# Blocks of seven products: one sum of weight quadrants moved from VectorE to an accumulating transfer within SBUF

## The chip, the cores and the metric

The kernel runs on one core of a Trainium2 chip. The metric is device time in microseconds (us): the median of three runs. One execution was also taken by the hardware profiler. In it TensorE (PE) multiplies, VectorE (DVE) and ScalarE (ACT) do elementwise work, GpSimd (POOL) does a little of that and issues its own transfers, and SyncE (SP) issues the loads from HBM. Each engine runs its instructions in order and waits for the others by semaphores.

## The reference, cut to what matters

Two layers of a hybrid model on 512 tokens of width 1024, in float32. Each layer has a mixer (a gated one in the first layer, attention with forgetting in the second, each beside attention to a memory) and then a feed-forward part, which is where the change lies:

```
a = rmsnorm(h, ln_ffn_pre[layer])
f = silu(a @ w_ffn_gate[layer]) * (a @ w_ffn_up[layer])      # 1024 -> 2816
h = h + rmsnorm(f @ w_ffn_down[layer], ln_ffn_post[layer])   # 2816 -> 1024
```

## The kernel before

**Products in three parts.** A float32 operand is split in two parts, `hi` (a cast on ScalarE) and `lo` (what the cast left, a subtraction on VectorE); both come from `split`, and all splits have line L239. A product is three matmuls (`mm3`, L191 to L193): hi by hi, hi by lo and lo by hi in such an order that the third, L193, is the first to need the weights' `wlo`.

**Blocks of seven.** Most of the feed-forward products are done by a Strassen-like scheme: a 2x2 product of quadrants takes seven products in place of eight, and some additions of quadrants for it. `Seven` does it for a block of 256 columns of the gate or up weights. Its four weight quadrants a11, a12, a21, a22 are the halves of two loaded tiles `raw` (512 KB each, in a pool of four; each quadrant is 128x512 and 256 KB). `sums` makes s3 = a11 + a21 (L1041), then a21 + a22 (L1043), then from it a11 + a21 + a22 (L1045), then the last sum in a12 (L1046), each in place but for s3, and splits a11 and a12 in between, while they hold what was loaded. Products 1 to 7 are then run in the order 1, 7, 2, 6, 4, 3, 5, with the further splits in between (`run`). Product 7 uses s3 and is written to the PSUM tile `e`; products 1, 5 and 6 go to `a`, 2 and 3 to `x`, 4 to `e`. At the end (`end`) VectorE joins the results out of PSUM (L1079, L1080, L1082), which also frees those tiles.

`DownSeven` does the same for the down weights, whose sums are L1205 (s3), L1207 and L1208; half of these blocks have tiles `raw`, half four tiles `wd` of 256 KB.

**Groups.** A layer's 22 slices of 128 columns of gate and up are done as one plain pair and five groups. A group has two gate blocks and two up blocks in the order gate, up, gate, up. In the first group of a layer the first two are run with products 1, 2, 3 of the gate block, then of the up block, then the rest (`plain_first`), and the sums of all four blocks stand close together. After each of the first four groups come two `DownSeven` in `down_sevens`: eight transfers that accumulate onto the result tiles `y` in SBUF (`put`, L1234), and additions by VectorE (L1262, L1265, L1268). In layer 0 the inner groups open at about 262, 326, 390 and 450 us, in layer 1 at 844, 908, 970 and 1030. The first block of the next group is prepared while a group's down blocks run, so that the splits and sums of the one and the additions of the other stand mixed on VectorE.

**What sets the order.** A scheduler sets the order of instructions on each engine by priorities and modelled times; it keeps what depends on what. POOL's queue holds its transfers in order: the accumulates onto `y`, and those that finish the low part of `flo` (L1153), which are also accumulates of 256 KB within SBUF.

Of the kernel before, what the change touches and what calls it, by code (L numbers as in the profile page):

```python
# [11 lines left out]
ALU = mybir.AluOpType  # L12
# [28 lines left out]
def hybrid(ctx: ExitStack, tc: tile.TileContext, i: dict, out: bass.AP):  # L41
# [13 lines left out]
    def name(s):  # L55
        n_of[s] = n_of.get(s, 0) + 1
        return f"{s}_{n_of[s]}"
# [4 lines left out]
    def plain(s, shape=(P, T), dt=F32):  # L62
        return yp.tile(list(shape), dt, tag="y", name=name(s))

    def prob(s, shape=(P, T)):
        return tp.tile(list(shape), F32, tag="p", name=name(s), bufs=6)

    def temp(s, shape=(P, T), tag="t", bufs=4, dt=F32):
        return tp.tile(list(shape), dt, tag=tag, name=name(s), bufs=bufs)
# [4 lines left out]
    def ps(tag, shape=(P, T), s="ps"):  # L74
        return pp.tile(list(shape), F32, tag=tag, name=name(s), bufs=2 if tag == "tr" else 3)

    V, A, PE, G = nc.vector, nc.scalar, nc.tensor, nc.gpsimd
# [63 lines left out]
    def loaded(src):  # L141

        raw = wp.tile([P, 1024], F32, tag="raw", name=name("raw"), bufs=4)
        last_load[0] = nc.sync.dma_start(raw, src)
        return raw
# [116 lines left out]
    class Norm:  # L262


        def __init__(self, width=T):
            self.r4 = small("r4")
            self.acc, self.width = None, width
# [26 lines left out]
        def sums(self, tb, cols):  # L294
            return [self.acc[:, c + tb * P : c + (tb + 1) * P] for c in range(0, T, self.width)]
# [722 lines left out]
    class Seven:  # L1018
# [5 lines left out]
        def __init__(self, xs, src, tag, rows):  # L1024
            self.xs, self.rows = xs, rows
            w1, w2 = loaded(src(0)), loaded(src(1))
            self.a = [w[:, d : d + 512] for w in (w1, w2) for d in (0, 512)]
            self.x, self.p = ps(tag, s="x"), ps(tag, (P, 256), s="a")
            self.q = ps(tag, (P, 256), s="e")
            self.s1, self.s2 = prob("s1"), prob("s2")  # L1030
# [6 lines left out]
        def sums(self):  # L1037

            a11, a12, a21, a22 = self.a
            self.s3 = temp("s3")  # L1040
            V.tensor_add(self.s3, a11, a21)  # L1041
            self.w1 = self.parts(a11)
            V.tensor_add(a21, a21, a22)  # L1043
            self.w2 = self.parts(a12)
            V.tensor_add(a11, a21, a11)  # L1045
            V.tensor_add(a12, a11, a12)  # L1046

        def product(self, o, w, n, more=False):
# [64 lines left out]
    def feed_forward(layer, phase, xp, meanwhile=None):  # L1113
# [41 lines left out]
        class Inner:  # L1155

            def __init__(self, aside):
                self.aside, self.u = aside, {}
# [23 lines left out]
        class DownSeven:  # L1182

            def __init__(self, k, spare):
                if spare:
                    self.a = [plain("wd").rearrange("p (m c) -> p m c", m=4) for _ in range(4)]
                    for n, a in enumerate(self.a):
                        last_load[0] = nc.sync.dma_start(
                            a, i["w_down"][layer, 4 * (n // 2) : 4 * (n // 2) + 4, :, k + n % 2, :].rearrange("m p c -> p m c"))
                else:  # L1190
                    raws = []
                    for dh in range(2):
                        raw = wp.tile([P, 1024], F32, tag="raw", name=name("raw"), bufs=4)
                        last_load[0] = nc.sync.dma_start(
                            raw.rearrange("p (m c) -> p m c", m=4),
                            i["w_down"][layer, 4 * dh : 4 * dh + 4, :, k : k + 2, :].rearrange("m p k c -> p m (k c)"))
                        raws.append(raw.rearrange("p (m k c) -> p m k c", m=4, k=2))
                    self.a = [r[:, :, x, :] for r in raws for x in range(2)]

            def sums(self, pair):  # L1200
                self.x = pair.x
                a11, a12, a21, a22 = self.a
                self.w = {2: a12, 4: a22}
                s3 = temp("s3").rearrange("p (m c) -> p m c", m=4)
                V.tensor_sub(s3, a11, a21)  # L1205
                self.w[1] = self.parts(a11)
                V.tensor_add(a21, a21, a22)  # L1207
                V.tensor_sub(a11, a11, a21)  # L1208
                self.w.update({5: a21, 6: a11, 7: s3})

            def parts(self, src, aside=False):
# [307 lines left out]
    with tc.tile_pool(name="ffn0", bufs=4) as xp:  # L1519
        phase = feed_forward(0, phase, xp, memory())  # L1520
    with tc.tile_pool(name="fox", bufs=1) as fp:
        phase = layer_b(phase, fp)
    with tc.tile_pool(name="ffn1", bufs=4) as xp:
        tail, ys = feed_forward(1, phase, xp)
# [97 lines left out]
```

## Time and profile before

| | us |
|---|---|
| Median of three runs (lowest, highest) | 1106.64 (1105.35, 1108.34) |
| The profiled execution | 1104.82 |
| Its span in the trace | 1103.1 |
| TensorE busy | 1082.6 (98%) |
| VectorE busy | 970.7 (88%) |
| ScalarE busy | 754.5 (68%) |
| POOL busy | 93.8 (9%) |

The profiled execution took 1.7 us more than its span, and lay 1.8 us under the median. A row of a timeline gives the start, the length, the engine, the line, what is written and read, and in brackets the idle time before it and what ended that. A row of waits gives who waited for whom: microseconds in all, times, and the longest.

### The profile page before, as it was taken

The numbers are of one execution on the slowest core, as the hardware profiler recorded it, in microseconds if no ns is written. First come the engines' busy times: TensorE is split into PE (matmuls) and PEld (weight loads), VectorE is DVE, ScalarE is ACT, GpSimd is POOL, SyncE is SP. The second block draws the span as 40 slices with busy tenths as digits, with TensorE's granted clock in tenths as the row PEclk, the third lists the DMA queues.
The fourth block names the chain that finished last, engine by engine and source line by source line (L and its number), as shares of the span: only waits on it lengthen the run. The fifth ranks groups of instructions, "written<-read, shape, count | busy, mean of one in ns | idle before, by whom it ended". The sixth has DMA issues, their size and how long they took to land.

```text
span 1103.1 us, 19756 instructions
## 1 busy us (share of the span) xinstructions
PE 1082.6 (98%) x7266; PEld 983.3 (89%) x7267; DVE 970.7 (88%) x1942; ACT 754.5 (68%) x1588; POOL 93.8 (9%) x120
## 2 busy tenths in 40 slices
PE   9999999999999999999999999999999999999998
PEld 7998889997979899998988998889997979899996
DVE  7879759998999999997968789868999989999986
ACT  7776578665756757677746788868666756756664
POOL 0000000002020201101000000000002020201100
PEclk9999999999999999999999999999999999999999
DMA  7521331338464664746222654531338464564722
GB/s 269 160 82 51 120 116 39 115 97 191 120 158 125 136 173 97 207 134 193 68 86 59 154 136 120 148 115 40 115 97 191 116 159 129 116 173 106 180 97 77
DMA packets 83992, 139.64 MB, mean 127 GB/s; under 512 B 6772, under 2 KB 49800, under 8 KB 83896
## 3 DMA queue, kind: packets, MB, share of 16 engines
q1 hardware_dynamic: 71480, 116.57, 34.4%
q0 software_dynamic: 11712, 21.50, 11.7%
q8 instruction: 57, 0.93, 0.4%
q10 hardware_dynamic: 704, 0.32, 0.1%
q14 instruction: 39, 0.32, 0.1%
HBM read 105.23 MB, written 2.10 MB: 97 GB/s over the span
## 4 chain that ended last, share of the span: by engine, by line
PE 85%; DVE 5%; DMA 5%; ACT 3%; issue 1%; SPq 1%; POOL 0%; DVEq 0%; ACTq 0%
PE a L193 5%; PE a L192 5%; PE a L191 5%; PE y L191 4%; PE y L193 4%; PE y L192 4%; PE ps L191 4%; PE ps L193 4%; PE ps L192 4%; DMA y<-yo 4%; PE e L193 3%; PE e L192 3%; PE e L191 3%; PE x L193 3%; PE x L192 3%; PE x L191 3%
## 5 line engine op out<-in xcount | busy, mean ns | idle before, releaser
L239 ACT CAST whi<-raw 128x512 fp32r<-128x512 f32 x444 | 260.7, 619 | 117.9 <-DVE raw L1045 58.2
L239 DVE TENSOR_TENSOR wlo<-raw,whi 128x512 fp32r<-128x512 f32 x444 | 290.6, 682 | 21.0 <-ACT whi L239 20.3
L193 PE MATMUL x<-xshi,wlo 128*128 128x256 f32 x320 | 90.4, 282 | 0.2 <-DVE wlo L239 0.2
L192 PE MATMUL x<-xslo,whi 128*128 128x256 f32 x320 | 90.1, 282 | 0.0
L191 PE MATMUL x<-xshi,whi 128*128 128x256 f32 x320 | 90.1, 282 | 0.0
L192 PE MATMUL a<-xslo,whi 128*128 128x256 f32 x320 | 89.9, 281 | 0.0
L191 PE MATMUL a<-xshi,whi 128*128 128x256 f32 x320 | 89.8, 281 | 0.0
L193 PE MATMUL a<-xshi,wlo 128*128 128x256 f32 x320 | 89.7, 281 | 0.0
L1234 POOL DMA_DIRECT2D y<-yo x64 | 55.5, 1143 | 196.9 <-ACT yo L1232 135.0
L191 PE MATMUL ps<-xshi,whi 128*128 128x256 f32 (+1 forms) x224 | 68.4, 306 | 0.0
L192 PE MATMUL ps<-xslo,whi 128*128 128x256 f32 (+1 forms) x224 | 66.7, 298 | 0.0
L193 PE MATMUL ps<-xshi,wlo 128*128 128x256 f32 (+1 forms) x224 | 66.3, 298 | 0.0
L239 ACT CAST whi<-s 128x512 fp32r<-128x512 f32 x56 | 34.7, 620 | 41.0 <-DVE s L1205 25.0
L193 PEld LDWEIGHTS x<-xshi,wlo 128*128 128x128 f32 x320 | 60.6, 189 | 0.4 <-DVE wlo L239 0.4
L191 PEld LDWEIGHTS a<-xshi,whi 128*128 128x128 f32 x320 | 60.2, 188 | 0.4
L192 PEld LDWEIGHTS a<-xslo,whi 128*128 128x128 f32 x320 | 60.2, 188 | 0.4
L192 PEld LDWEIGHTS x<-xslo,whi 128*128 128x128 f32 x320 | 60.5, 189 | 0.0
L191 PEld LDWEIGHTS x<-xshi,whi 128*128 128x128 f32 x320 | 60.5, 189 | 0.0
L193 PEld LDWEIGHTS a<-xshi,wlo 128*128 128x128 f32 x320 | 60.2, 188 | 0.0
L193 PE MATMUL e<-t3hi,wlo 128*128 128x256 f32 x160 | 45.7, 286 | 10.5 <-DVE wlo L239 10.5
L191 PE MATMUL y<-whi,mixedhi 128*128 128x512 f32 x128 | 51.3, 401 | 0.0
L192 PE MATMUL y<-wlo,mixedhi 128*128 128x512 f32 x128 | 50.6, 395 | 0.0
(352 smaller groups left out, 3637.4 us busy)
## 6 DMA issues: line engine op xcount, KB each, us to landing
raw<-in_w_gate SPq DMA_DIRECT2D x44, 512.0 KB, 3.7
raw<-in_w_up SPq DMA_DIRECT2D x44, 512.0 KB, 5.3
y<-yo POOLq DMA_DIRECT2D x64, 256.0 KB, 5.8
raw<-in_w_down SPq DMA_DIRECT2D x28, 512.0 KB, 4.6
raw<-in_w_out SPq DMA_DIRECT2D x16, 512.0 KB, 4.0
wd<-in_w_down SPq DMA_DIRECT2D x32, 256.0 KB, 8.8
flo<-s POOLq DMA_DIRECT2D x16, 256.0 KB, 5.1
raw<-in_w_b_q SPq DMA_DIRECT2D x8, 512.0 KB, 4.4
```

The costliest lines, as they stand in the source:

```text
L191: PE.matmul(o, w[0], x[0], start=start, stop=False, skip_group_check=more)
L192: PE.matmul(o, w[0], x[1], start=False, stop=False, skip_group_check=more)
L193: return PE.matmul(o, w[1], x[0], start=False, stop=stop, skip_group_check=more)
L239: last_parts[:] = A.copy(hi, src), (eng or V).tensor_sub(lo, src, hi)
L1234: G.dma_start(ys[tb][dh], some, accum_op=ALU.add)
```

## The change

In both kinds of block the sum a21 + a22 is no longer made by VectorE. A transfer issued by POOL, with addition, puts a22 onto a21 within SBUF, as soon as both loads have landed. s3 is then not a11 + a21, since a21 no longer holds what was loaded: VectorE first makes a11 + a21 + a22 in a11, after a11's split, and takes a22 from it. In `DownSeven` the same is done with its signs.

```diff
@@ class Seven, __init__
             w1, w2 = loaded(src(0)), loaded(src(1))
             self.a = [w[:, d : d + 512] for w in (w1, w2) for d in (0, 512)]
+            G.dma_start(self.a[2], self.a[3], accum_op=ALU.add)
@@ sums
             self.s3 = temp("s3")
-            V.tensor_add(self.s3, a11, a21)
             self.w1 = self.parts(a11)
-            V.tensor_add(a21, a21, a22)
+            V.tensor_add(a11, a21, a11)
+            V.tensor_sub(self.s3, a11, a22)
             self.w2 = self.parts(a12)
-            V.tensor_add(a11, a21, a11)
             V.tensor_add(a12, a11, a12)
@@ class DownSeven, __init__
+                G.dma_start(self.a[2], self.a[3], accum_op=ALU.add)
@@ sums
-                V.tensor_sub(s3, a11, a21)
                 self.w[1] = self.parts(a11)
-                V.tensor_add(a21, a21, a22)
                 V.tensor_sub(a11, a11, a21)
+                V.tensor_add(s3, a11, a22)
```

In the changed kernel the transfer of `Seven` is L1028, a11 + a21 + a22 is L1043, s3 is L1044, and the last sum stays L1046; the transfer of `DownSeven` is L1199. VectorE has 56 instructions fewer, one for each block, and POOL issues 56 transfers more.

The scheduler moves work with it. The opening of the third group of layer 0 on VectorE, before; `raw_53` and `raw_54` are the first gate block's tiles, `wlo_149` and `wlo_150` the low parts of a11 and a12, `wlo_151` that of s3, `ys` and `yc` results of the down blocks:

```order
L1041 TENSOR_TENSOR s3_13_4112<-raw_53_4103,raw_54_4105 128x512
L239 TENSOR_TENSOR wlo_149_4115<-raw_53_4103,whi_149_4114 128x512
L1043 TENSOR_TENSOR raw_54_4105<-raw_54_4105 128x512
L1265 TENSOR_TENSOR y_26_2472<-ys_3_3929,y_26_2472 128x512
L1265 TENSOR_TENSOR y_28_2474<-ys_4_3930,y_28_2474 128x512
L239 TENSOR_TENSOR wlo_150_4120<-raw_53_4103,whi_150_4119 128x512
L1045 TENSOR_TENSOR raw_53_4103<-raw_54_4105,raw_53_4103 128x512
L1268 TENSOR_TENSOR y_29_2475<-yc_3_3927,y_29_2475 128x512
L1268 TENSOR_TENSOR y_31_2477<-yc_4_3928,y_31_2477 128x512
L1046 TENSOR_TENSOR raw_53_4103<-raw_53_4103 128x512
L239 TENSOR_TENSOR wlo_151_4139<-s3_13_4112,whi_151_4138 128x512
```

And the same place after:

```order
L239 TENSOR_TENSOR wlo_149_4115<-raw_53_4103,whi_149_4114 128x512
L239 TENSOR_TENSOR wlo_150_4121<-raw_53_4103,whi_150_4120 128x512
L1043 TENSOR_TENSOR raw_53_4103<-raw_54_4105,raw_53_4103 128x512
L1265 TENSOR_TENSOR y_26_2472<-ys_3_3930,y_26_2472 128x512
L1044 TENSOR_TENSOR s3_13_4113<-raw_53_4103,raw_54_4105 128x512
L1265 TENSOR_TENSOR y_28_2474<-ys_4_3931,y_28_2474 128x512
L1046 TENSOR_TENSOR raw_53_4103<-raw_53_4103 128x512
L239 TENSOR_TENSOR wlo_151_4139<-s3_13_4113,whi_151_4138 128x512
L1268 TENSOR_TENSOR y_29_2475<-yc_3_3928,y_29_2475 128x512
L1268 TENSOR_TENSOR y_31_2477<-yc_4_3929,y_31_2477 128x512
```

Behind the second L1265, five operations stood ahead of the split of s3, and now one does. The fourth and fifth groups have the same order. In the second group it is L1043, L1265, L1265, L1044, L1046, L1268, L1268 and then the split of s3, so that four stand there. On TensorE, at all these openings, the first two matmuls of `e` were followed by five of `x` and then by the other ten of `e`; now the twelve of `e` stand together, and the twelve of `x` behind them.

The third block of the first group of layer 0 on VectorE, before; `raw_37` and `raw_38` are that block's tiles, and L1079 belongs to the end of the group's first block:

```order
L1041 TENSOR_TENSOR s3_3_2853<-raw_37_2844,raw_38_2846 128x512
L239 TENSOR_TENSOR wlo_80_2861<-raw_37_2844,whi_80_2860 128x512
L1043 TENSOR_TENSOR raw_38_2846<-raw_38_2846 128x512
L1045 TENSOR_TENSOR raw_37_2844<-raw_38_2846,raw_37_2844 128x512
L239 TENSOR_TENSOR wlo_81_2880<-s3_3_2853,whi_81_2879 128x512
L1046 TENSOR_TENSOR raw_37_2844<-raw_37_2844 128x512
L239 TENSOR_TENSOR wlo_82_2909<-raw_37_2844,whi_82_2908 128x512
L1041 TENSOR_TENSOR s3_4_2990<-raw_39_2981,raw_40_2983 128x512
L1079 TENSOR_TENSOR s2_1_2551<-e_1_2549,s2_1_2551 128x256
```

And after:

```order
L239 TENSOR_TENSOR wlo_80_2863<-raw_37_2845,whi_80_2862 128x512
L1043 TENSOR_TENSOR raw_37_2845<-raw_38_2847,raw_37_2845 128x512
L1044 TENSOR_TENSOR s3_3_2855<-raw_37_2845,raw_38_2847 128x512
L1046 TENSOR_TENSOR raw_37_2845<-raw_37_2845 128x512
L239 TENSOR_TENSOR wlo_81_2881<-s3_3_2855,whi_81_2880 128x512
L1079 TENSOR_TENSOR s2_1_2552<-e_1_2550,s2_1_2552 128x256
```

The order of the sums is the new one, and L1043, the first that needs the transfer's result, stands four operations ahead of L1079.

POOL's queue after, from the end of the first group of layer 0 to the second block of the second (before, it holds the rows of L1153 and L1234 alone):

```order
L1153 DMA flo_5_2823<-s2_2_2615 128x512
L1028 DMA raw_44_3325<-raw_44_3325 128x512
L1234 DMA y_25_2471<-yo_1_3194 128x512
L1234 DMA y_27_2473<-yo_2_3197 128x512
L1234 DMA y_26_2472<-yo_3_3210 128x512
L1234 DMA y_30_2476<-yo_3_3210 128x512
L1234 DMA y_28_2474<-yo_4_3214 128x512
L1234 DMA y_32_2478<-yo_4_3214 128x512
L1234 DMA y_30_2476<-yo_5_3271 128x512
L1234 DMA y_32_2478<-yo_6_3274 128x512
L1028 DMA raw_46_3462<-raw_46_3462 128x512
L1199 DMA wd_7_3618<-wd_8_3619 128x512
```

The transfer for a group's first block (`raw_44`) stands ahead of the eight onto `y`, that for its second block (`raw_46`) behind all eight.

## The prediction

> **What bounds the kernel now.** I read the page first, then TensorE's waits, then the table of the stretches, then the timeline of the places that these pointed to.
>
> ```profile
> span 1103.1 us, 19756 instructions
> PE 1082.6 (98%) x7266; PEld 983.3 (89%) x7267; DVE 970.7 (88%) x1942; ACT 754.5 (68%) x1588; POOL 93.8 (9%) x120
> PE 85%; DVE 5%; DMA 5%; ACT 3%; issue 1%; SPq 1%; POOL 0%; DVEq 0%; ACTq 0%
> PE e L193 <- DVE wlo L239: 10.5, 6, 2.4
> 195.00:258.00 63.00, 62.68 (x433) 57.21 (x432) 60.69 (x113) 43.98 (x89) 7.14 (x8) 1.00 0.46 116
> 258.00:320.00 62.00, 59.46 (x413) 55.06 (x412) 57.28 (x103) 38.53 (x78) 8.09 (x10) 0.97 0.54 137
> 320.00:382.00 62.00, 60.20 (x422) 55.48 (x422) 59.41 (x108) 40.22 (x81) 8.90 (x11) 1.00 0.58 145
> 444.00:498.00 54.00, 53.95 (x428) 52.44 (x427) 52.83 (x96) 35.84 (x76) 2.00 (x3) 1.00 0.58 168
> ```
>
> TensorE is busy for 1082.6 of 1103.1 us, so no more than 20.5 us can be had by anything that leaves its matmuls alone, and this change does. VectorE is busy for 88%; its work is worth something only where TensorE waits for it. The fourth line names such a place: six times, 10.5 us in all, product 7 (written to `e`) waited at its third matmul, the first that needs `wlo` of s3. The stretches (columns: length, then busy time of PE, PEld, DVE, ACT, POOL, the granted clock, the DMA share, GB/s) show where. In 195 to 258 us, the first group of layer 0, TensorE never really waits; in an inner group it loses about 2 us of 62; in the last group nothing. VectorE has 2 to 5 us to spare in a group.
>
> The place itself, in the third group (rows of VectorE, then of TensorE):
>
> ```profile
> 326.35 0.69 DVE L1265 TENSOR_TENSOR y<-ys,y 128x512 f32<-128x512 f32 x1 [2.14 <-PE yc L193]
> 326.96 0.68 DVE L239 TENSOR_TENSOR wlo<-raw,whi 128x512 fp32r<-128x512 f32 x1
> 327.56 0.68 DVE L1045 TENSOR_TENSOR raw<-raw,raw 128x512 f32<-128x512 f32 x1
> 328.16 1.28 DVE L1268 TENSOR_TENSOR y<-yc,y 128x512 f32<-128x512 f32 x2
> 329.36 0.68 DVE L1046 TENSOR_TENSOR raw<-raw 128x512 f32<-128x512 f32 x1
> 329.96 0.68 DVE L239 TENSOR_TENSOR wlo<-s,whi 128x512 fp32r<-128x512 f32 x1
> 328.34 0.28 PE L192 MATMUL e<-t3lo,whi 128*128 128x256 f32 x1
> 328.45 0.28 PE L191 MATMUL x<-xshi,whi 128*128 128x256 f32 x1
> 330.69 0.38 PE L193 MATMUL e<-t3hi,wlo 128*128 128x256 f32 x1 [1.49 <-DVE wlo L239]
> ```
>
> VectorE's second L1265 waits until 326.35, five more operations stand between it and the split of s3 (`wlo<-s`), and TensorE, after five matmuls of `x` that fill 0.58 us, stops until 330.69. What L1265 waits for is an accumulate of `y` by POOL's queue; in the second group the chain shows it, and the page gives that queue's latencies (L1234, then L1153):
>
> ```profile
> 254.14 8.80 DMA y<-yo
> 263.04 0.69 DVE y L1265
> 267.39 0.39 PE e L193
> 267.77 0.12 PE e L191
> 269.08 0.21 PE x L191
> L1234 POOL DMA_DIRECT2D y<-yo x64: 832/1007/1882, 248.6 to 1033.2; - x64
> DMA to landing us min/median/max: 3.3/5.8/11.3
> DMA to landing us min/median/max: 3.2/5.1/6.2
> ```
>
> **The change, part by part.** *VectorE's work.* Each of 56 blocks (40 of gate and up, 16 of down) loses one 128x512 addition. Such operations follow each other by 0.60 us (326.96 to 327.56), so 33.6 us leave VectorE. This is not the gain; TensorE waited 10.5 us for it at these places, and only there does it count.
>
> *The openings of inner groups.* There the order counts more than the operation. In the third, fourth and fifth group of a layer, the new order puts s3 between the two L1265, and behind the second only L1046 and the split of s3. The split then starts 2 x 0.60 us after 326.35 where it started 3.61 us after, so 2.4 us earlier. TensorE's order loses its filler of five `x` matmuls, so it reaches the third `e` 0.58 us earlier and must then do them; it would arrive at 328.46 (0.12 after 328.34), and the split ends at 328.23 (326.35 + 1.20 + 0.68). The whole wait goes: the five matmuls from 328.45 end at 329.04, so 1.6 us to 330.69. The other openings:
>
> ```profile
> 392.47 0.39 PE L193 MATMUL e<-t3hi,wlo 128*128 128x256 f32 x1 [1.48 <-DVE wlo L239]
> 848.55 0.39 PE L193 MATMUL e<-t3hi,wlo 128*128 128x256 f32 x1 [1.46 <-DVE wlo L239]
> 911.63 0.38 PE L193 MATMUL e<-t3hi,wlo 128*128 128x256 f32 x1 [2.38 <-DVE wlo L239]
> 973.41 0.39 PE L193 MATMUL e<-t3hi,wlo 128*128 128x256 f32 x1 [1.53 <-DVE wlo L239]
> ```
>
> By the same count (a bracket is about 0.15 short of the gap between starts, as the model lets a matmul run on): 1.6 at 330 and at 392, 1.7 at 973, and at 911 some 1.9 of a larger wait. In the second group (267 and 848) both L1265 stand ahead of s3, and only one operation fewer lies between: 0.60 earlier, less 0.58 of lost filler, so nothing. The fifth group has no such wait. Sum: -6.8 us. Ends: 0, if another landing holds VectorE there, and -8.4, if also the slow stretch below goes.
>
> That stretch: behind the 267.39 wait the `x` matmuls follow each other by 0.21 us where `e` took 0.12, and the granted clock of 258 to 320 is 0.97; some 1.6 us were lost by it. No other of the six waits had such a sequel. The wait stays about as long, so I take 0; were it gone, or come to a second opening, that is 1.6 less or more. The Trainium skill, TensorE: Matmul & The Clock Gate, Part 1, says that the clock is halved after an idle window of a free-running 3.4 us clock. By that rule a wait of 2.2 us should not have done it, the stretch has another cause and stays, and the sum is the same; the trace puts it right behind the wait, hence the 1.6 to both sides.
>
> *The first group of a layer.* Here the accumulate is not covered. The third block's second load lands at 214.4, as L1041 shows, which waited for it:
>
> ```profile
> 214.44 0.69 DVE L1041 TENSOR_TENSOR s<-raw,raw 128x512 f32<-128x512 f32 x1 [0.46 <-DMA raw<-in_w_gate]
> 219.38 0.41 DVE L1079 TENSOR_TENSOR s<-e,s 128x256 f32<-128x256 f32 x1
> 796.37 0.69 DVE L1041 TENSOR_TENSOR s<-raw,raw 128x512 f32<-128x512 f32 x1 [0.56 <-DMA raw<-in_w_gate]
> 211.32 1.53 SPq L144 DMA_DIRECT2D raw<-in_w_up  x2
> raw<-in_w_up SPq DMA_DIRECT2D x44, 512.0 KB, 5.3
> 220.82 0.28 PE L191 MATMUL a<-xshi,whi 128*128 128x256 f32 x1
> ```
>
> Then POOL starts the accumulate and VectorE's next row, L1043, waits for it. No row shows the accumulate of a weight quadrant; the nearest is that of `flo`, also 256 KB within SBUF and outside the bursts, at 3.2, 5.1 and 6.2 us (least, median, most). The next block's two loads, issued from 211.32 and by their median some 5 us under way, are still moving, so I take the median: it lands at T = 219.6 (217.7 to 220.7). The Trainium skill, DMA: Bandwidth & Descriptors, Anatomy of one DMA, fits 2.0 us plus bytes by 436 GB/s; estimated from it 2.6 us for 256 KB, which is under every row here, and by it the first group would lose nothing. Behind the waiting L1043 on VectorE stand L1044, L1046, the split of s3 and L1079, which frees the PSUM tile into which TensorE writes `a` from 220.82. L1079 would end at T + 4 x 0.60 + 0.41, so TensorE is late by T - 218.0: 1.6 us (0 to 2.7). VectorE waited for the same load in layer 1, at 796.37. Sum: +3.2 (0 to 5.4).
>
> *The second blocks of inner groups.* POOL's queue is in order, and the new accumulate stands behind the eighth accumulate of `y`. That issue, VectorE's arrival, and TensorE's need in the third and in the fifth group:
>
> ```profile
> 329.25 0.86 POOL L1234 DMA_DIRECT2D y<-yo  x1 [3.53 <-ACT whi L239]
> 332.97 0.68 DVE L1041 TENSOR_TENSOR s<-raw,raw 128x512 f32<-128x512 f32 x1
> 451.39 0.86 POOL L1234 DMA_DIRECT2D y<-yo  x1 [3.11 <-ACT whi L239]
> 455.03 0.68 DVE L1041 TENSOR_TENSOR s<-raw,raw 128x512 f32<-128x512 f32 x1
> 462.20 0.28 PE L193 MATMUL e<-t3hi,wlo 128*128 128x256 f32 x1
> ```
>
> It can be issued 0.95 after, and by the median of `flo` lands at T = 335.3 in the third group, so VectorE waits 2.3 us. Product 7 needs T + 2.75 (four rows and a wait of ScalarE's cast) and comes 7.2 after L1041, less the 1.6 won: 338.6. That is covered by 0.5. In the fifth, beside the loads of the last group, I take the slowest `flo`, T = 458.5, and 461.3 against 462.20 is in time. But VectorE has no time to spare there (52.83 of 54): 3.5 us of waiting less four saved rows of 0.60 make it 1.1 late, of which I take half, +0.6 (0 to 2). With all eight at the slowest, each of the others would miss by some 0.6.
>
> *The rest.* The third and fourth blocks of inner groups have loads 5 to 9 us ahead of VectorE, and the down blocks as much; an accumulate of 6 us is covered there, though not of 10. The 56 transfers add 14 MB of reads and as much of writes within SBUF; beside a DMA share of 0.4 to 0.6 I cost this at nothing, since TensorE waits for loads nowhere but in the first group. POOL's own 56 issues of about 1 us stand in 9% of busy time.
>
> Sum: -6.8 + 3.2 + 0.6 = -3.0 us, against 1104.8 (the profiled execution; the span and 1.7). That execution lies 1.8 under the median of 1106.6, so the forecast against the median is 1103.6.
>
> **Rivals.** *Accumulates late everywhere* (slower). Place: L1043 at the head of VectorE's queue in the second blocks and in the first groups. Price: the first groups at their upper end, 5.4, and the eight second blocks 1 us each, 8, less 6.8: +6.6, 1113.2. It decides once the accumulate within SBUF takes over about 6 us, which could be, since its reads and writes both load the ports. For it speaks the 10 us in bursts of L1234; against, that lone ones took 3.2 and 3.3 with the same bytes.
>
> *No change.* The openings are won and given back: either the first `y` accumulates land later, since another accumulate now is in the queue, so that openings keep half their wait (-3.4 in place of -6.8), or the first groups cost 5.4 in place of 3.2. That gives +0.4 or -0.8, 1106.4 in the middle. For it speaks that the wait for `y` heads the chain; against, that the order of POOL puts none of the new ones between the first and the eighth `y`.
>
> *A larger gain.* The accumulate takes 3.2 and costs the first groups nothing, and the slow clock of the second group is not met: -6.8 - 1.6, 1098.2. For it speaks the quiet latency; against, the loads in flight at 214.
>
> **How the numbers follow.** About 0.3%, 3.3 us, is what a measurement of this kernel can tell from no change. My forecast of -3.0 with its own spread (-6 to 0) has 0.50, 0.24 of it beyond the 0.3%; the larger gain 0.17, no change 0.15, late accumulates 0.18. So faster 0.24 + 0.17 = 0.41, slower 0.18 and 0.02 from the edge of no change, 0.20, same 0.39. The range for 8 in 10 reaches from 1098 (the larger gain) to 1109.5, half way into the slow rival.
>
> **What would show it.** Right: L1041 and 56 VectorE rows are gone (about 936 us busy); the waits of `e` for `wlo` fall from 10.5 us to about 5, the second group's alone; in 195 to 258 VectorE's L1043 waits 4 to 5 us for DMA and TensorE loses 1 to 2 us at `a`; the accumulates of L1028 land in 3.3 to 6 us. Wrong: waits for DMA at L1043 in many blocks with TensorE idle at `e` behind them, latencies over 6 us, `y` landing later than before in the openings, or more stretches with a granted clock under 1.

## The result, and the profile after

The changed kernel took 1132.80 us (median of 4 runs, 1130.26 to 1136.51) against 1105.99 before (4 runs): ratio 1.0242, 95% interval 1.0208 to 1.0276. It is 27 us slower where 3.0 us less was forecast. The page, after (the last row is POOL's transfers: packets, MB, share of 16 DMA engines), and the same last row of the page before:

```profile
span 1130.3 us, 19985 instructions
PE 1094.8 (97%) x7267; PEld 987.4 (87%) x7267; DVE 946.0 (84%) x1886; ACT 746.1 (66%) x1588; POOL 144.4 (13%) x176
PE 53%; DVE 21%; DMA 9%; ACT 9%; issue 7%; POOL 1%; SPq 1%; DVEq 0%; ACTq 0%; POOLq 0%
q0 software_dynamic: 22848, 36.18, 19.5%
```

```profile
q0 software_dynamic: 11712, 21.50, 11.7%
```

VectorE did get less to do, 946.0 us for 970.7, and yet its share of the chain that ended last went from 5% to 21%. The waits after, of TensorE and of VectorE, with the latency of L1028:

```profile
PE e L191 <- ACT whi L239: 8.0, 6, 2.7
PE e L191 <- ACT s L1074: 4.7, 4, 1.2
PE e L193 <- DVE wlo L239: 3.9, 8, 2.3
DVE raw L1043 <- issue: 29.3, 6, 6.5
DVE raw L1043 <- DMA raw<-raw: 11.6, 4, 4.2
DMA to landing us min/median/max: 3.2/3.4/7.9
```

L1043 is the first operation that needs the transfer. VectorE stood still in front of it for 40.9 us in ten places. Six of them are put down to "issue"; in each, L1043 starts 0.08 us after the last semaphore event of its transfer, so they are waits for the transfer too, and all six are second blocks of inner groups. Of the other four, two are the third blocks of the first groups and two are third blocks in layer 1. The second block of the second group of layer 0 (POOL, then VectorE, then TensorE):

```profile
266.77 0.84 POOL L1234 DMA_DIRECT2D y<-yo  x1 [3.66 <-ACT whi L239]
269.93 0.85 POOL L1028 DMA_DIRECT2D raw<-raw  x1 [2.32 <-DMA wd<-in_w_down]
267.24 3.70 DVE L239 TENSOR_TENSOR wlo<-raw,whi 128x512 fp32r<-128x512 f32 x6
277.46 0.69 DVE L1043 TENSOR_TENSOR raw<-raw,raw 128x512 f32<-128x512 f32 x1 [6.52 <-issue]
279.62 0.69 DVE L239 TENSOR_TENSOR wlo<-s,whi 128x512 fp32r<-128x512 f32 x1
277.04 0.28 PE L193 MATMUL a<-xshi,wlo 128*128 128x256 f32 x1
279.64 0.39 PE L191 MATMUL e<-t3hi,whi 128*128 128x256 f32 x1 [2.32 <-ACT whi L239]
280.72 0.42 PE L191 MATMUL e<-t3hi,whi 128*128 128x256 f32 x1
280.94 0.41 PE L192 MATMUL e<-t3lo,whi 128*128 128x256 f32 x1
```

The transfer is issued at 269.93 and lands 7.5 us later. VectorE, through with its splits at 270.9, waits 6.5 us; TensorE ends product 1 at 277.2 and stops until 279.64 for s3. Behind the stop its matmuls follow each other by 0.22 us in place of 0.12: the granted clock was halved from 280.4 to 283.8.

To see where the 27 us arose I took the start of the same matmul in both traces, after minus before, at the first product of the blocks of the inner groups (us):

| layer, group | block 1 | block 2 | block 3 | block 4 |
|---|---|---|---|---|
| 0, second | 2.89 | -0.93 | 3.90 | 3.96 |
| 0, third | 4.54 | 2.77 | 5.66 | 5.64 |
| 0, fourth | 6.37 | 4.54 | 9.77 | 9.69 |
| 0, fifth | 10.31 | 10.21 | 13.44 | 13.51 |
| 1, second | 17.20 | 15.71 | 19.80 | 19.79 |
| 1, third | 20.48 | 21.54 | 23.23 | 23.32 |
| 1, fourth | 24.39 | 22.61 | 25.52 | 25.56 |
| 1, fifth | 26.47 | 26.88 | 26.95 | 26.86 |

Read along a row. The first block wins (-9.3 over eight groups), the second loses (+24.9), the third nothing. What a second block loses goes with the time that its transfer takes to land: 4.1 to 5.2 us where that is 7.5 to 7.9 us, 2.9 to 3.2 where it is 6.3 to 6.5, and 0.1 where it is 4.5. In the third group of layer 1 it is 4.3; the 1.7 us lost there come from the third block's transfer, which took 6.6. From a row's end to the next row's start lie the fourth block and the down blocks, 0.6 to 1.1 us in six places, and between the layers 3.7.

### The profile page after: what moved, and what is told of

Its sections match the earlier page's. It is cut to its first block, busy times and chain, and to the rows that moved or that the text cites. A ratio compares the mean times of both kernels' runs of the same rounds, so it can differ in the third digit from the quotient of the medians.

```text
span 1130.3 us, 19985 instructions
## 1 busy us (share of the span) xinstructions
PE 1094.8 (97%) x7267; PEld 987.4 (87%) x7267; DVE 946.0 (84%) x1886; ACT 746.1 (66%) x1588; POOL 144.4 (13%) x176
## 3 DMA queue, kind: packets, MB, share of 16 engines
q1 hardware_dynamic: 71480, 116.57, 33.5%
q0 software_dynamic: 22848, 36.18, 19.5%
## 4 chain that ended last, share of the span: by engine, by line
PE 53%; DVE 21%; DMA 9%; ACT 9%; issue 7%; POOL 1%; SPq 1%; DVEq 0%; ACTq 0%; POOLq 0%
DVE wlo L239 8%; ACT whi L239 5%; PE y L191 4%; PE y L192 4%; PE y L193 4%; PE ps L191 4%; PE ps L193 4%; PE ps L192 4%; DMA y<-yo 3%; DMA raw<-raw 2%; PE v L191 2%; PE v L192 2%; PE v L193 2%; DMA wd<-in_w_down 2%; PE a L191 1%
## 5 line engine op out<-in xcount | busy, mean ns | idle before, releaser
L239 DVE TENSOR_TENSOR wlo<-raw,whi 128x512 fp32r<-128x512 f32 x444 | 287.5, 683 | 26.7 <-ACT whi L239 24.6
L1234 POOL DMA_DIRECT2D y<-yo x64 | 54.9, 1134 | 137.2 <-ACT yo L1232 72.6
L1028 POOL DMA_DIRECT2D raw<-raw x40 | 35.5, 888 | 218.1 <-DVE s L1044 50.8
L1043 DVE TENSOR_TENSOR raw<-raw,raw 128x512 f32<-128x512 f32 x40 | 27.4, 685 | 41.8 <-issue 29.3
L191 PE MATMUL e<-t3hi,whi 128*128 128x256 f32 x160 | 46.5, 291 | 8.7 <-ACT whi L239 8.0
```

What stands on the lines that cost most here:

```text
L191: PE.matmul(o, w[0], x[0], start=start, stop=False, skip_group_check=more)
L239: last_parts[:] = A.copy(hi, src), (eng or V).tensor_sub(lo, src, hi)
L1028: G.dma_start(self.a[2], self.a[3], accum_op=ALU.add)
L1234: G.dma_start(ys[tb][dh], some, accum_op=ALU.add)
```

## The experiments

The first theory, W: VectorE waits at the head of its queue for the late transfer of the second block. The rivals: C, the traffic of 56 more transfers slows everything that lands; S, the new order of the sums costs the time. Each ratio below is to the kernel before, timed along with the run; its median lay between 1105.2 and 1107.8 us.

**The second blocks back on VectorE.** The edit, cut; `moved` is false in the second block of an inner group and true elsewhere:

```diff
-            G.dma_start(self.a[2], self.a[3], accum_op=ALU.add)
+            if moved:
+                G.dma_start(self.a[2], self.a[3], accum_op=ALU.add)
...
             self.w1 = self.parts(a11)
+            if not self.moved:
+                with behind(last_parts[1:]):
+                    V.tensor_add(a21, a21, a22)
```

> The changed kernel, but in the second block of each of the eight inner groups VectorE makes a21 + a22 itself, at the place in its queue just ahead of L1043; the sums keep their new order and the other 48 blocks keep the transfer. Theory W (VectorE waits at the head of its queue for the late transfer of the second block): from the shift between the two traces those blocks cost about 25 us, so 1108 us (1104 to 1112). Rival C (the traffic of 56 more transfers slows all that lands): 8 of 56 are gone, 27 x 48/56, so about 1129. Rival S (the new order of the sums, s3 last, costs the time): order unchanged, 1131 to 1136.

Measured 1123.22 us, ratio 1.0128 (1.0076 to 1.0181): 10 us came back by the medians and 13 by the ratios, between W and C, and no theory had named that. The trace shows why (VectorE, TensorE, then VectorE's waits):

```profile
282.82 0.69 DVE L1047 TENSOR_TENSOR raw<-raw,raw 128x512 f32<-128x512 f32 x1 [3.23 <-issue]
285.21 0.39 PE L191 MATMUL a<-xshi,whi 128*128 128x256 f32 x1 [1.43 <-ACT s L1075]
DVE raw L1047 <- DMA raw<-raw: 24.3, 7, 4.1
```

The second block no longer waits. The third now does: its transfer was issued at 276.42, when its load had landed, and took 6.3 us. The wait had only moved on by one block. So W was too narrow, and theory D took its place: around an opening the DMA engines are full, and any accumulate there takes 6 to 8 us, whichever block it serves.

**No transfer at all, the new order of the sums kept.** VectorE makes a21 + a22 behind the split of a11, in all 56 blocks.

> All 56 blocks: new order of the sums (s3 from the sum over three), but VectorE makes a21 + a22 and there is no new transfer; VectorE has as many instructions as before. At the openings six operations stand between the second y addition and the split of s3, where five stood before. W and C: no late transfer, no traffic; one operation more at the openings, up to 8 x 0.6, so 1106 to 1112. S: over 1125.

Measured 1111.25 us, ratio 1.0036 (1.0025 to 1.0047), inside what W and C expected; S falls. What this form costs by itself is 4 us, not 27. At the openings the scheduler's order is not quite that of the changed kernel (in the third group both additions L1268, L1270 there, stand ahead of s3), so this run tests the order of the sums and not every move of the scheduler.

**The two kinds of block apart.** The edit undoes the diff in one class.

> The change in the 16 down blocks alone; the 40 gate and up blocks as before. W: their loads land long before VectorE comes, nobody waits: 1104 to 1109. C: 16 of 56 transfers, so about 8 us slower, 1114.

Measured 1104.40 us, ratio 0.9967 (0.9953 to 0.9982): the down blocks' part alone is slightly faster, and its 16 transfers, whose loads are early, hurt nobody.

> The change in the 40 gate and up blocks alone. The scheduler then puts the split of s3 behind both additions L1268 at all openings, so the won 1.6 us waits come back. W: the second blocks wait as in the changed kernel: 1130 to 1138. C: 40 of 56 transfers, 27 x 40/56, so about 1125.

Measured 1130.31 us, ratio 1.0204 (1.0183 to 1.0226): nearly the whole loss is in the gate and up blocks, as W (and D) say.

**The engines relieved at the openings.** The `wd` loads of a down block fell into the opening. Here they are issued behind the loads of the group's fourth block:

```diff
-                    if m > k0:
-                        downs.append(DownSeven(m, True))
                 sevens(...)
+                if gi < len(groups) - 1 and m > k0:
+                    downs.append(DownSeven(m, True))
...
+                    with behind([last_load[0]]):
                         for n, a in enumerate(self.a):
```

> The changed kernel, but the four wd loads of a down block (256 KB each, which fell into the opening of a group and are needed some 50 us later) are queued on SP behind the loads of the group's fourth block; nothing else is moved by hand. Theory D (the DMA engines are full around an opening, so the second and third blocks' accumulates land after 6.5 to 8 us where a lone one takes 3.3, and VectorE waits for them): 1 MB leaves that stretch, the accumulates land some 4 us sooner, most of the waits at L1043 go, 1110 us (1104 to 1117). Rival Q (the accumulates are late because POOL's own queue runs them one behind the other, after the eight of y): 1128 to 1135.

Measured 1123.81 us, ratio 1.0162 (1.0144 to 1.0179): 9 us back, less than half of what D expected, and under Q's range. Times from issue to landing, first of the transfer that had taken 7.5 us in the second group, then of the third block of the first group, here and, last, in the changed kernel:

```profile
DMA to landing us min/median/max: 3.7/3.7/3.7
DMA to landing us min/median/max: 7.3/7.3/7.3
DMA to landing us min/median/max: 4.4/4.4/4.4
```

In the relieved opening the accumulate takes 3.7 us. In the first group, where the new place of the `wd` loads put them beside the third block's accumulate, it takes 7.3 in place of 4.4. The same loads, moved, moved the latency both ways: that is D. The fall is not the loads' alone, since the edit takes that down block's own accumulate along (L1199, issued 2.8 us behind the second block's in the changed kernel and 18 us behind it here); beside the rise, and in the control that follows, there is no such accumulate. D was not complete either: in the fourth and fifth group of layer 0 the second block's accumulate still took 6.2 and 7.6 us.

> The control: the kernel before with the same four wd loads moved. D: the accumulates of y at the openings land sooner, and part of the 10.5 us of waits for the split of s3 goes: 1099 to 1105 us. Q: no change, 1104 to 1109.

The control did more than D asked: 1093.16 us, ratio 0.9886 (0.9868 to 0.9904). This kernel contains nothing of the change. Its waits for the split of s3 went from 10.5 us to 2.0 (TensorE). In the second group, for one, the second L1266 (L1265 before) now starts 2.3 us earlier, 0.9 of it because the whole group opens earlier (VectorE):

```profile
PE e L193 <- DVE wlo L239: 2.0, 2, 1.1
260.78 0.69 DVE L1266 TENSOR_TENSOR y<-ys,y 128x512 f32<-128x512 f32 x1 [1.48 <-DMA y<-yo]
```

The accumulates of `y` landed after 4.4 us in the median, where they took 5.8 before. With the waits the halved stretch at 268 us is gone as well (granted clock 1.00 from 250 to 270 us).

> The changed kernel with the wd loads moved behind the fourth block's loads in the inner groups alone; the first group keeps its order, where the earlier kernel had put the wd loads beside the third block's accumulate (7.3 us there in place of 4.4, and 3.5 us lost in each layer). D: those 7 us come back: 1117 us (1113 to 1120). Q: 1123 to 1135.

Measured 1117.68 us, ratio 1.0105 (1.0068 to 1.0142): the first groups' share came back as expected, though the runs spread from 1110.6 to 1122.8.

> The kernel before with the wd loads moved in the inner groups alone. No accumulate is waited for in its first group, so all as with the loads moved in every group: 1093 us (1091 to 1096).

Measured 1094.61 us, ratio 0.9896 (0.9865 to 0.9928), as expected.

**The transfers chosen by place.** The same edit as in the first experiment, with other blocks in the condition.

> The transfer only where its load is long there: first and fourth blocks of a group and the first group's first two, and all down blocks; VectorE makes a21 + a22 in the second and third blocks, and in the first group's third. Order of the sums as in the changed kernel. W and D alike: no late accumulate is waited for, and the openings keep what they won (their waits for the split of s3 are gone): 1098 to 1104 us. If it is the number of transfers in all (C): 34 of 56 are left, about 1122.

Measured 1096.02 us, ratio 0.9909 (0.9891 to 0.9928), under the range. The transfers left are 38 and not 34, which I had miscounted; no wait of VectorE for one of them is in the list, and the openings keep what they won.

> The transfer only in the first block of each group and in the down blocks; VectorE makes a21 + a22 in all others. D: the fourth blocks' transfers were covered, so as the kernel with first and fourth, within 3 us, 1098 to 1105; C: 26 of 56 transfers are left, about 1118.

Measured 1100.67 us, ratio 0.9950 (0.9934 to 0.9966): in the range, though 4.7 us behind the kernel with first and fourth where 3 were expected, so the transfers of the fourth blocks (with those of the first groups' second blocks) gain as well.

> The transfer only in the second blocks of the eight inner groups and in the down blocks; VectorE makes the sum in the other 32 gate and up blocks. D: these eight are the ones that wait; with 24 of 56 transfers, 8 x 2 to 3 us, 1124 us (1115 to 1128), while 26 transfers in the other places gave 1101. C (their number): 27 x 24/56 over before, 1117 at most, and no more than the kernel with 26.

Measured 1127.63 us, ratio 1.0201 (1.0154 to 1.0249). This settles C: 24 transfers, eight of them in second blocks, cost 21 us, while 26 and 38 transfers, none of them in a second block of an inner group, gain 5 and 9 (ratios 0.9950 and 0.9909). The waits, of VectorE with the second blocks alone, and of TensorE with first and fourth blocks:

```profile
DVE raw L1047 <- issue: 25.5, 6, 6.3
PE e L193 <- DVE wlo L239: 2.6, 3, 1.3
```

> The kernel with the transfer in first and fourth blocks and down blocks, and the wd loads moved in the inner groups. Both took the same waits away (those of the openings), so their 9 and 12 us do not add: D says 1091 us (1088 to 1094), somewhat under the better of the two.

Measured 1099.15 us, ratio 0.9936 (0.9917 to 0.9954): a miss. It is no better than the first of its two parts, and 4.5 us slower than the second, timed along with it. The waits for s3 stand at 2.9 us, where the first part alone had 2.6, so there was nothing left there to win twice; that I had expected some 2 us less than the better part shows that I added without a wait to take it from. Why it is slower than its second part was not followed up. Best of all is the kernel before with the loads moved, 1093.2 us.

## Why the prediction was wrong

**The step that failed is "The second blocks of inner groups"**, the term of +0.6 us. It measured +24.9 us, 1.7 of it through a third block's transfer. The mechanism stood in the text, the new accumulate behind the eighth of `y` and VectorE in front of L1043; its size was wrong in two ways: the landing, and what follows a late landing.

The latency was taken from `flo`, 5.1 us and 6.2 at most. None of the 16 `flo` transfers took 5.1: eight took 3.3 to 4.4 us, with a DMA share of 0.44 to 0.61 over their flight, and eight 5.7 to 6.2, with 0.87 to 0.94, so the median lies between two kinds. At the opening it was 6.3 to 7.9 us in six of the eight, with a share of 0.98 to 1.09 over the flight. (The other two took 4.3 and 4.5 at 0.97 and 0.87, so the share is not all of it.) The text judged the load by the shares of whole groups, 0.54 and 0.58. The same view in stretches of 4 us, before, then after:

```profile
254.00:258.00 4.00, 3.70 (x16) 3.03 (x17) 4.00 (x8) 3.49 (x7) 2.53 (x3) 1.00 1.06 199
258.00:262.00 4.00, 4.00 (x19) 3.23 (x18) 1.87 (x3) 0.62 (x1) 0.84 (x1) 1.00 1.08 270
262.00:266.00 4.00, 3.17 (x24) 2.80 (x22) 2.96 (x5) 1.03 (x2) 0.50 (x1) 1.00 1.11 301
266.00:270.00 4.00, 2.61 (x17) 2.62 (x18) 4.00 (x8) 2.90 (x7) 0.36 (x1) 0.83 0.62 110
257.00:261.00 4.00, 4.00 (x19) 3.23 (x18) 4.00 (x7) 3.77 (x8) 1.83 (x3) 1.00 0.99 199
265.00:269.00 4.00, 4.00 (x31) 3.75 (x30) 4.00 (x7) 4.00 (x9) 0.84 (x1) 1.00 1.07 324
273.00:277.00 4.00, 4.00 (x36) 4.00 (x35) 0.00 (x0) 0.00 (x0) 0.53 (x1) 1.00 1.03 244
```

The share before the GB/s is 1.06 to 1.11 from 254 to 266 us already in the kernel before: the engines were full, and this could have been read. After, they are full until 277, with the accumulate at the end of that. The Trainium skill, DMA: Bandwidth & Descriptors, Issuing engines are not separate DMA queues, says that transfers of all engines run on the same 16 and interleave. The moved loads agree, with 3.7 us in place of 7.5 for POOL's accumulate in the relieved opening.

And a wait of VectorE is paid twice, of which the prediction had only the first payment, at product 7. In the second and the fourth group of layer 0, product 7 came 2.5 and 2.9 us late, and behind that stop the clock was halved for 3.4 us, which costs some 1.7 us more; the latter is in the profile's table:

```profile
390.00:456.00 66.00, 62.35 (x423) 56.79 (x422) 56.09 (x100) 39.33 (x81) 14.13 (x16) 0.97 0.69 160
```

In the other four late second blocks, two in each layer, TensorE stopped again for 1.2 us, at product 4. In the third group of layer 0 (ScalarE, then TensorE):

```profile
348.81 0.63 ACT L1135 ACTIVATE s<-s 128x512 f32<-128x512 f32 x1 [1.96 <-DVE s L1134]
349.35 0.35 ACT L1074 COPY s<-e 128x256 f32<-128x256 f32 x1
349.76 0.38 PE L191 MATMUL e<-t,whi 128*128 128x256 f32 x1 [1.17 <-ACT s L1074]
```

There the accumulate landed at 340.98, and the third matmul of product 7 came 1.0 us late, close to the 0.8 that the prediction's own sum gives for such a landing. The rest of the 2.9 us came behind: VectorE, held up, reached L1134 late, ScalarE waited for it in L1135, and the copy L1074 behind that one, which frees `e` for product 4, came late too.

The other steps:

- *VectorE's work*: 56 rows gone, right; busy time fell by 24.7 us and not by 33.6. The lengths of all its rows together fell by 35; the busy time counts overlapping ends once, and fewer rows overlap now.
- *The openings*, -6.8: measured -9.3. The third and fourth groups of layer 0 and the fourth of layer 1 won 1.8 each, as worked out. The second groups won 3.8 and 1.5 where I had nothing; in layer 0 the slow-clock stretch went and L1265 waited less. The third group of layer 1 lost 1.1 where I had -1.9: its second L1265 waited 4.2 us for `y` (3.5 before), so the stop in front of `wlo` of s3 stayed at 2.5 us, and this time a halved stretch of 3.4 us followed. That the sum is near the forecast is therefore in part luck.
- *The first groups*, +3.2: about +2.4 (1.5 and 0.9); the accumulate took 4.4 and 3.8 us where I took 5.1.
- *The rest*, 0: the down blocks became longer by 0.6 to 1.1 us in each group, some 7 us in all. TensorE waits there for ScalarE's `b` and `yo`, 3.3 us in all, which the kernel before did not; the rest was not found. The kernel with the down blocks alone has the same waits for `b` (2.8 us, eight times), so those come from the down blocks' new order or their transfers; which of these was not tried.
- *The rival that came nearest* is "Accumulates late everywhere", which had a chance of 0.18. Its place was right for the second blocks, though not for the first groups, and its 6 us parts the six late blocks from the other two; its price of 1 us a block was a third of the 3.1 measured.

Sum: 0.3 before the first group, 2.4 first groups, -9.3, +24.9, 7 in the down blocks and 1.7 between the layers make 27; the spans differ by 27.2.

What stays open: how the 6 to 8 us divide between waiting behind POOL's own accumulates of `y` and sharing the engines with loads. Moving 1 MB of loads (with one accumulate) took nearly all of it away in the second group of layer 0 and none in the fifth, where 6.5 us became 7.6. An accumulate into a spare tile, for which nobody waits, would have shown the traffic alone; it was not tried.

## What to carry to other kernels

Before work is moved from an engine to a transfer, read the DMA share at that very place, in stretches of a transfer's length, and price the transfer by a row from there; a mean over a stage hides engines that are full. Then ask what stands behind the first instruction that needs it: an engine that runs in order turns a late transfer into a wait of everything behind. And when a stop of the busiest engine ends in a transfer, look at what else is under way: moving loads that nobody needed yet was worth 12 us here, more than any form of the change that was tried.

## What was not expected of the hardware

An accumulate within SBUF is dear for its size: POOL's queue took 11.7% of 1103.1 us before and 19.5% of 1130.3 after, 91.3 us of all 16 engines for 56 transfers, 1.6 us for 256 KB each. The queue of the loads took 34.4% of 1103.1 us for 116.57 MB, which is 1.7 us for 512 KB. A lone one agrees, with a share of 0.47 over the 3.25 us from 309.65. As the profile counts it, one such accumulate occupies the engines as long as a load of twice its bytes.

The clock was halved three times within the changed kernel, each time for 3.4 us by the granted clock: behind stops of TensorE of 2.5, 2.9 and 2.5 us, and not behind those of 1.6 and 1.7 us. The length of the stop alone does not decide it. In the kernel before, the stop that ended at 267.39 us (2.4 us long) had such a stretch behind it, and the one that ended at 911.63 (2.5 us) had none; nor had one of 2.9 us at 1032.48 in the kernel with the down blocks alone. The Trainium skill, TensorE: Matmul & The Clock Gate, Part 1, asks for an idle window of 3.4 us; the traces here differ from that, since all of these stops are shorter.
